# Modulation pieces and the latent attention's first projections take turns behind the recurrence

## The chip, the cores and the metric

The kernel runs on one core of one Trainium2 chip. The core's engines each work through a program of their own in order: TensorE (PE, the matmuls), VectorE (DVE), ScalarE (ACT), GpSimd (POOL) and SyncE (SP), whose queue issues the DMA transfers. They wait for each other through semaphores. The metric is the device time of one execution in microseconds (us), lower is better; the time of a kernel is the median of its runs.

## The reference

The reference is a trunk of two layers over 512 latent tokens and 256 context tokens of width 1024, in float32. Each layer normalises the tokens, scales and shifts them by a modulation vector, projects them once, gives the columns to four mixers, projects their outputs back and ends in a mixture of experts:

```python
for l in range(DEPTH):
    mod = sc @ w_ada[l] + b_ada[l]            # modulation, 6 * 1024 columns; modc likewise
    h = rmsnorm(x, norm1_g[l]) * (1 + s1) + sh1
    p = jnp.split(h @ w_in[l], split_at, axis=-1)
    o_a, oc_a = hgrn_mixer(p[0], ..., p[4], ...)           # gated recurrence, both directions
    o_b = hyena_mixer(p[5], *hy_args)                      # long convolution
    o_c, oc_c = na_mixer(p[6], ...)                        # neighbourhood attention
    o_d, oc_d = mla_mixer(p[7], p[8], p[9], ...)           # latent attention
    x = x + g1 * (jnp.concatenate([o_a, o_b, o_c, o_d], axis=-1) @ w_out[l])
    x = x + g2 * moe_ffn(rmsnorm(x, norm2_g[l]) * (1 + s2) + sh2, ...)
```

The change concerns three of these: the modulation `mod`, the recurrence `hgrn_mixer`, and the first projections of the latent attention, p[7] (256 columns) and p[8] (128 columns).

## The kernel before

The kernel is written in program order in Python; a scheduler then orders each engine's instructions. It keeps to what is written first where it can and fills gaps with what is written later, so the text sets priorities, and the order in which pieces are written sets the order in which they take up tiles of a shared pool.

**The recurrence** (`hgrn`). For two pairs of heads it first makes score tiles (L244), then goes through six levels. In a level, for each pair, ScalarE copies keys and queries into block order (L265), TensorE multiplies them (L237, 64-row matmuls into two large PSUM tiles `pa`), VectorE merges the result under a mask (L246) and multiplies the queries by the running decay (L272, L275), and POOL does the same with the keys (L273). The two pairs alternate. This is called the level loop below. Behind it, for each pair in turn, TensorE transposes the keys (L286) and multiplies them by the values (L299), VectorE runs a chain of 44 dependent small operations that carries the state over the blocks (L310, the state chain), and only then TensorE can make the outputs (L319, L322). The sum of squares (L328), ScalarE's square root by logarithm and exponential, and VectorE's last product (L332) close the pair. The result is written to memory by SP (`spill`).

**A modulation piece** (`Ada.step`, L1194). One of 24 column blocks of a layer's `mod`: two halves, each a 512 KB weight load that SP issues into a ring of three buffers (`araw`) and 4 small matmuls, which leave a 32-row result in a PSUM tile `pw`; ScalarE copies it out (L1199). After every eighth piece four matmuls sum the parts (L1204), VectorE adds the bias (L1209) and SP writes the row to memory (L1211). A half's load can be issued only when the half three before it has been multiplied.

**A projection** (`Proj.cols`, L1300). SP loads a 512 KB block of 128 columns (L1291), ScalarE rounds it to its high part (L1275), POOL makes the low part (L1276). TensorE multiplies high by high, high by low and low by high: 24 wide matmuls over the 512 latent tokens and, where the context is needed, 24 narrow ones over its 256 tokens. Each result is a PSUM tile `pw`; there are two such tiles, shared with the pieces, and they are given out in the order in which the code is written. Weight parts have two buffers. After each projection `between` adds the pieces that the list `STEPS` (layer 0) or `STEPS1` (layer 1) names for its number; behind the recurrence these are one piece after each of the projections named `cq`, `ckv` and the first three named `u` in layer 0, and none in layer 1.

In the code before, behind the call of `hgrn` stands `more(STEPH1 if l else STEPH)`: ten pieces in layer 0, thirteen in layer 1. Then come the projections `cq` (two) and `ckv` of the latent attention, which in layer 1 take `cq` over the latent tokens alone, and after them the six projections `u` of the long convolution.

Of the kernel before, what the change touches and what calls it, by code (L numbers as in the profile page):

```python
# [1347 lines left out]
ARAW1 = 3  # L1348
B0 = 1
STEPS1 = [1] * 2  # L1350
STEPH1 = 13
HLM = 2
FIRST = (12, 16)
FLIGHT = 5
LAG = 2
AHEAD = 1
STEPS = [1] * 8 + [0] * 2 + [1] * 6
STEPH = 10
CHUNK = 2048


# [41 lines left out]
def trunk(tc, d, out):  # L1403
# [7 lines left out]
    with ExitStack() as top:  # L1411
# [84 lines left out]
        def more(n, late=0):  # L1496
            for _ in range(n):
                if not adas[0].step(aring) and (l or late or adas[1].done < 8):
                    if adas[1].step(aring) and adas[1].done == 8:
                        adas[1].cols(n1g[1], mcs[1], mcb[1])  # L1500

        for l in range(2):
# [63 lines left out]
            def spill(group, tiles):  # L1566
                for k, o in enumerate(tiles):
                    nc.sync.dma_start(od[l][2 * group + k], o[:, :NQ])
# [1 line left out]
            E.cur = hg  # L1570
            ho = out_tiles()
            hgrn(E, full, QQ, F, K, V, SG, gn[:, 0:1], ho)
            more(STEPH1 if l else STEPH)
            spill(0, ho)


# [2 lines left out]
            ckv = E.t("mckv", NTOK, bufs=1)  # L1579
            for i in range(2):  # L1580
                pr.cols(COL["cq"] + i, both, lambda ps, a, n: nc.scalar.copy(cq[i][:, a:a + n], ps))
            pr.cols(COL["ckv"], PARTS, lambda ps, a, n: nc.scalar.copy(ckv[:, a:a + n], ps))
            hg.close()


# [194 lines left out]
            for c in range(4):  # L1780
# [3 lines left out]
                for t in range(nt + LAG * (c == 3)):  # L1784
                    if t < nt:
                        tt, cc = slice(t * P, (t + 1) * P), slice(c * 256, c * 256 + 256)
                        ps = E.pw()
                        i = 0
# [164 lines left out]
```

## Time and profile before

| | us |
|---|---|
| median of 3 runs | 2409.76 |
| lowest and highest run | 2402.96, 2412.77 |
| the profiled execution | 2422.56 |
| its span in the trace | 2420.7 |
| TensorE busy | 2043.4 (84%) |
| VectorE busy | 994.1 (41%) |
| level loop of layer 0 | 64.69 |
| from there to the end of the first projection `u` over the latent tokens | 52.65 |
| level loop of layer 1 | 46.86 |
| from there to the first third of the same projection | 51.48 |

The profiled execution took 12.8 us more than the median, so a difference worked out from its rows is applied to the median. The last four lines are the stretches in which the order of instructions changes. They are bounded by TensorE's instructions: the level loop goes from its first scores in a row to the first transposes of keys (L286). In rows of the timeline, xN counts TensorE's instructions as the profile does, and these matmuls take two each for the pieces and the recurrence.

### The profile page before, as it was taken

The numbers are of one execution on the slowest core, as the hardware profiler recorded it, in microseconds if no ns is written. First come the engines' busy times: TensorE is split into PE (matmuls) and PEld (weight loads), VectorE is DVE, ScalarE is ACT, GpSimd is POOL, SyncE is SP. The second block draws the span as 40 slices with busy tenths as digits, with TensorE's granted clock in tenths as the row PEclk, the third lists the DMA queues.
The fourth block names the chain that finished last, engine by engine and source line by source line (L and its number), as shares of the span: only waits on it lengthen the run. The fifth ranks groups of instructions, "written<-read, shape, count | busy, mean of one in ns | idle before, by whom it ended". The sixth has DMA issues, their size and how long they took to land. (4 is left out here: it accounts for less than half of the span.)

```text
span 2420.7 us, 32212 instructions
## 1 busy us (share of the span) xinstructions
PE 2043.4 (84%) x11540; PEld 1190.1 (49%) x11540; DVE 994.1 (41%) x2435; ACT 572.0 (24%) x1138; POOL 539.5 (22%) x429
## 2 busy tenths in 40 slices
PE   5789999899999588887777598999899598877776
PEld 1458688765688233322222386685669333222221
DVE  6751754647746422222112427555683511111111
ACT  3433432244622100000000234324351100000000
POOL 1652413211013122211111225131102221211111
PEclk9999899999998799999999799999998699999998
DMA  6434443202243899999999535520243899999996
GB/s 246 160 120 177 162 144 121 94 9 69 85 143 123 305 381 382 409 396 408 398 399 406 184 96 171 183 72 18 87 134 113 313 398 409 411 406 410 409 407 253
DMA packets 139310, 581.52 MB, mean 240 GB/s; under 512 B 23984, under 2 KB 47873, under 8 KB 88630
## 3 DMA queue, kind: packets, MB, share of 16 engines
q1 hardware_dynamic: 124054, 555.89, 59.5%
q0 software_dynamic: 15008, 22.36, 3.9%
q8 instruction: 151, 2.47, 0.4%
q14 instruction: 97, 0.79, 0.1%
HBM read 554.17 MB, written 36.80 MB: 244 GB/s over the span
## 5 line engine op out<-in xcount | busy, mean ns | idle before, releaser
L1012 PE MATMUL pb<-side,arena 128*64 128x512 f32 x1224 | 287.2, 603 | 42.7 <-DMA side<-in_w_moe 39.2
L1012 PE MATMUL pb<-arena 128*64 128x512 f32 x920 | 217.1, 604 | 36.5 <-DMA arena<-in_w_moe 33.0
L1016 DVE COPY arena<-pb 128x512 f32<-128x512 f32 x67 | 46.3, 691 | 490.7 <-PE pb L1012 490.7
L1028 ACT ACTIVATE arena<-pb 128x256 f32<-128x256 f32 x67 | 25.8, 384 | 899.9 <-PE pb L1025 899.9
L1276 POOL TENSOR_TENSOR wl<-side,wh 128x1024 fp32r<-128x1024 f32 x52 | 126.7, 2437 | 380.7 <-ACT wh L1275 252.1
L1012 PEld LDWEIGHTS pb<-side,arena 128*64 128x64 f32 x1224 | 81.7, 137 | 241.7 <-issue 128.9
L1300 PE MATMUL pw<-hh,wh 128*128 128x512 f32 (+1 forms) x720 | 166.1, 364 | 2.6 <-ACT arena L1644 1.3
L1043 DVE SCALAR_TENSOR_TENSOR arena<-pb,arena 128x512 f32<-128x512 f32 x67 | 50.3, 751 | 270.8 <-PE pb L1039 260.6
L1300 PE MATMUL pw<-hl,wh 128*128 128x512 f32 (+1 forms) x720 | 161.1, 358 | 0.0
L1039 PE MATMUL pb<-side,arena 128*64 128x512 f32 x576 | 140.5, 625 | 23.8 <-DVE arena L1029 22.0
L1300 PE MATMUL pw<-hh,wl 128*128 128x512 f32 (+1 forms) x720 | 159.0, 355 | 0.0
L1012 PEld LDWEIGHTS pb<-arena 128*64 128x64 f32 x920 | 61.9, 138 | 185.3 <-issue 99.5
L1052 POOL DMA_INDIRECT acc<-arena x35 | 55.2, 1578 | 385.8 <-DVE arena L1047 339.0
L1300 PEld LDWEIGHTS pw<-hh,wh 128*128 128x128 f32 x720 | 118.8, 191 | 35.1 <-issue 11.8
L1039 PE MATMUL pb<-arena 128*64 128x512 f32 x496 | 115.8, 606 | 23.5 <-DVE arena L1029 20.7
L1300 PEld LDWEIGHTS pw<-hh,wl 128*128 128x128 f32 x720 | 117.3, 189 | 25.8 <-issue 10.5
L1300 PEld LDWEIGHTS pw<-hl,wh 128*128 128x128 f32 x720 | 117.7, 189 | 24.6 <-issue 8.9
L1052 POOL DMA_INDIRECT out_dram<-arena x32 | 50.9, 1590 | 311.0 <-DVE arena L1043 296.9
L990 POOL DMA_INDIRECT arena<-h2d,arena x67 | 69.9, 1043 | 187.7 <-issue 75.6
L1795 POOL TENSOR_TENSOR arena<-arena 128x256 f32<-128x256 f32 x40 | 31.3, 783 | 301.1 <-DVE arena L1794 293.3
L1039 PEld LDWEIGHTS pb<-side,arena 128*64 128x64 f32 x576 | 39.7, 141 | 102.7 <-issue 60.7
L1025 PE MATMUL pb<-ident,arena 128*128 128x128 f32 x268 | 42.3, 280 | 55.4 <-DVE arena L1016 55.4
(367 smaller groups left out, 3442.5 us busy)
## 6 DMA issues: line engine op xcount, KB each, us to landing
side<-in_w_moe SPq DMA_DIRECT2D x215, 1024.0 KB, 13.6
arena<-in_w_moe SPq DMA_DIRECT2D x169, 1024.0 KB, 13.4
arena<-in_w_ada SPq DMA_DIRECT2D x53, 512.0 KB, 3.6
side<-in_w_in SPq DMA_DIRECT2D x52, 512.0 KB, 3.5
side<-in_w_ada SPq DMA_DIRECT2D x43, 512.0 KB, 4.0
arena<-in_w_out SPq DMA_DIRECT2D x16, 512.0 KB, 5.0
arena<-in_x SPq DMA_DIRECT2D x12, 512.0 KB, 5.6
spd<-arena SPq DMA_DIRECT2D x23, 256.0 KB, 2.4
```

What stands on the lines that cost most here:

```text
L990: E.gathered = nc.gpsimd.indirect_dma_start(out=xg, out_offset=None, in_=h2d, in_offset=bass.IndirectOffsetOnAxis(ap=gi, axis=0), **(dict( ...
L1012: nc.tensor.matmul(pg[64 * s:64 * s + 64], xT[:, j // 4, j % 4, :], W[j // 2][:, (j % 2) * 1024 + s * 512:(j % 2) * 1024 + s * 512 + 512], ...
L1016: nc.vector.tensor_copy(gu, pg)
L1025: nc.tensor.transpose(pt[:, c * 128:(c + 1) * 128], gu[:, c * 128:(c + 1) * 128], E.c["ident"])
L1028: nc.scalar.activation(hT, pv[:, :, 0, :], AF.Silu)
L1039: nc.tensor.matmul(pd[64 * s:64 * s + 64], hT[:, c, :], W[4 + c // 2][:, (c % 2) * 1024 + s * 512:(c % 2) * 1024 + s * 512 + 512], start=( ...
L1043: nc.vector.scalar_tensor_tensor(y, pd, w[0], g2[0], op0=ALU.mult, op1=ALU.mult)
L1052: E.nc.gpsimd.indirect_dma_start(out=acc, out_offset=bass.IndirectOffsetOnAxis(ap=si, axis=0), in_=y, in_offset=None, compute_op=ALU.add, ...
L1276: (nc.vector if k % 2 else nc.gpsimd).tensor_sub(lo, src, hi.bitcast(F32))
L1300: nc.tensor.matmul(ps[:, :n], w[:, j, :], h[:, j, a:a + n], start=(i == 0), stop=(i == 23))
L1795: nc.gpsimd.tensor_add(x1[t][:, cc], x1[t][:, cc], tmp)
```

## The change

After `hgrn` no piece is written any more. Instead the pieces stand behind the three projections of the latent attention: 3, 3 and 4 in layer 0, 4, 4 and 5 in layer 1. With those of `STEPS` that is 4, 4 and 5 in both layers. The number of pieces, of projections and of everything else stays the same.

```diff
-STEPH1 = 13
-STEPH = 10
+STEPH = ((3, 3, 4), (4, 4, 5))
...
             hgrn(E, full, QQ, F, K, V, SG, gn[:, 0:1], ho)
-            more(STEPH1 if l else STEPH)
             spill(0, ho)
...
             for i in range(2):
                 pr.cols(COL["cq"] + i, both, lambda ps, a, n: nc.scalar.copy(cq[i][:, a:a + n], ps))
+                more(STEPH[l][i])
             pr.cols(COL["ckv"], PARTS, lambda ps, a, n: nc.scalar.copy(ckv[:, a:a + n], ps))
+            more(STEPH[l][2])
             hg.close()
```

Outside the two stretches every engine's order is the same as before; from the next projection on TensorE's rows are identical.

On TensorE, in the level loop of layer 0 (`pa` are the recurrence's score tiles, L1194 a piece, L1300 a projection with `wh`, `wl` its weight parts and `hh`, `hl` the parts of the tokens), this is the middle of the loop:

```order
+L1300 MATMUL pw_2215<-hh_502,wl_2212 128x512
+L1300 MATMUL pw_2241<-hh_502,wh_2211 128x256 x6
+L237 MATMUL pa_1704<-arena 128x128 x4
+L237 MATMUL pa_1705<-arena 128x128 x4
 L237 MATMUL pa_1704<-arena 128x128
 L237 MATMUL pa_1705<-arena 128x128
-L1194 MATMUL pw_2268<-side_343,csil 32x256 x5
+L237 MATMUL pa_1704<-arena 128x128
+L237 MATMUL pa_1705<-arena 128x128
+L1300 MATMUL pw_2241<-hh_502,wh_2211 128x256 x2
+L1300 MATMUL pw_2241<-hl_503,wh_2211 128x256 x6
```

Between the scores of two levels there now stand matmuls of the first `cq` projection where a piece stood. In the whole loop ten pieces and a sum with 9 wide matmuls of `cq` became all of the first `cq`, four pieces and 7 wide matmuls of the second. In the loop of layer 1 nine pieces and a sum became the 24 wide matmuls of the first `cq`, four pieces and 2 wide matmuls of the second.

On TensorE behind the loop of layer 0, for the second pair of heads, this stood between the products of keys and values (L299) and the outputs (L319, L322) that need the state chain:

```order
L299 MATMUL pa_2080<-arena 128x64 x12
L299 MATMUL pa_2119<-arena 128x64 x12
L1300 MATMUL pw_2482<-hl_503,wh_2478 128x512
L1300 MATMUL pw_2482<-hh_502,wl_2479 128x512 x8
L1300 MATMUL pw_2508<-hh_502,wh_2478 128x256 x8
L1300 MATMUL pw_2508<-hl_503,wh_2478 128x256 x8
L1300 MATMUL pw_2508<-hh_502,wl_2479 128x256 x8
L1194 MATMUL pw_2534<-arena,csil 32x256 x4
L1194 MATMUL pw_2534<-side_343,csil 32x256 x4
L1300 MATMUL pw_2553<-hh_502,wh_2549 128x512 x8
L1300 MATMUL pw_2553<-hl_503,wh_2549 128x512 x5
L319 MATMUL pa_2158<-arena 64x128
```

and this stands there now:

```order
L299 MATMUL pa_2080<-arena 128x64 x12
L299 MATMUL pa_2119<-arena 128x64 x12
L1300 MATMUL pw_2434<-hl_503,wh_2430 128x512 x2
L1300 MATMUL pw_2434<-hh_502,wl_2431 128x512 x8
L1300 MATMUL pw_2460<-hh_502,wh_2430 128x256 x8
L1300 MATMUL pw_2460<-hl_503,wh_2430 128x256 x8
L1300 MATMUL pw_2460<-hh_502,wl_2431 128x256 x8
L1194 MATMUL pw_2486<-side_343,csil 32x256 x8
L1194 MATMUL pw_2498<-arena,csil 32x256 x4
L319 MATMUL pa_2158<-arena 64x128
L322 MATMUL pa_2158<-arena 64x64 x2
L319 MATMUL pa_2158<-arena 64x128
```

The 13 wide matmuls of the first `u` projection went behind the pair's outputs, and half a piece and one wide matmul of `ckv` came in. Behind the outputs there now stand three and a half pieces in a row, and then `u`. For the first pair the matmuls in this place are 14 wide and 24 narrow ones of the second `cq` with one and a half pieces; for the two pairs of layer 1 they are 18 wide matmuls, two pieces and a sum, and then one wide and 24 narrow matmuls with two pieces. In layer 1 before, the first of these places held three pieces and most of a sum, and nothing else.

On POOL, in layer 1 (L273 is the recurrence's product of the keys, by level; L1276 the low part of a projection's weights), the level loop now holds one weight split:

```order
 L273 TENSOR_TENSOR arena<-arena 128x96x4 x4
 L273 TENSOR_TENSOR arena<-arena 128x48x8 x4
+L1276 TENSOR_TENSOR wl_16934<-side_15490,wh_16933 128x1024
 L273 TENSOR_TENSOR arena<-arena 128x24x16 x4
 L273 TENSOR_TENSOR arena<-arena 128x12x32 x4
-L1276 TENSOR_TENSOR wl_17003<-side_15490,wh_17002 128x1024
 L1276 TENSOR_TENSOR wl_17062<-side_15490,wh_17061 128x1024
 L1276 TENSOR_TENSOR wl_17095<-side_15490,wh_17094 128x1024
```

The split of `ckv` moved from behind the loop to the place between two of its levels. The same happens in layer 0, and ScalarE's rounding of the same weights (L1275) moves with it. On SP, in layer 1, the load of the projection weights that reuses this block's buffer moved ahead of the pieces' loads of the loop.

## Rows read from the trace of the kernel before

**Rows 1.** The page, its first line: the span of the profiled execution.

```profile
span 2420.7 us, 32212 instructions
```

**Rows 2.** Windows: from:to, length, busy PE, PEld, DVE, ACT, POOL, clock, DMA share, GB/s.

```profile
242.72:307.41 64.69, 58.73 (x561) 43.96 (x561) 50.99 (x77) 25.20 (x63) 27.50 (x33) 0.87 0.51 176
...
307.41:360.06 52.65, 52.12 (x481) 42.33 (x479) 28.06 (x97) 20.52 (x33) 7.59 (x3) 1.00 0.33 111
...
1465.36:1512.22 46.86, 39.59 (x410) 27.08 (x409) 40.44 (x77) 20.13 (x60) 27.63 (x33) 0.93 0.60 199
...
1512.22:1563.70 51.48, 46.19 (x400) 33.90 (x397) 28.01 (x99) 18.14 (x34) 7.39 (x3) 0.97 0.46 155
```

**Rows 3.** Timeline of VectorE, layer 0's level loop: start, length, [idle before <-releaser].

```profile
266.04 1.94 DVE L246 COPY_PREDICATED arena<-hmask,pa 128x768 f32<-128x768 uint32 x2 [1.36 <-PE pa L237]
...
281.56 1.94 DVE L246 COPY_PREDICATED arena<-hmask,pa 128x768 f32<-128x768 uint32 x2 [4.23 <-PE pa L237]
...
298.26 0.68 DVE L1209 TENSOR_TENSOR arena<-pw,arena 128x512 f32<-128x512 f32 x1
```

**Rows 4.** Timeline of TensorE, layer 0's level loop: two of its waits.

```profile
257.07 3.63 PE L237 MATMUL pa<-arena 64*128 64x128 f32 x24 [1.78 <-DVE arena L246]
...
277.66 0.62 PE L1194 MATMUL pw<-side,csil 128*32 128x256 f32 x2 [3.30 <-DMA side<-in_w_ada]
```

**Rows 5.** Timeline behind layer 0's loop: TensorE, and VectorE's state chain.

```profile
309.61 2.90 PE L299 MATMUL pa<-arena 64*128 64x64 f32 x48
...
311.22 11.15 DVE L310 SCALAR_TENSOR_TENSOR arena<-arena,pa 64x64 f32<-64x64 f32 x44 [3.24 <-PE pa L299]
...
324.21 0.27 PE L322 MATMUL pa<-arena 128*64 128x64 f32 x1
...
327.29 1.20 PE L1300 MATMUL pw<-hh,wl 128*128 128x512 f32 x4
```

**Rows 6.** Timeline of TensorE, layer 0: a piece, then a projection's halves.

```profile
373.50 1.07 PE L1194 MATMUL pw<-side,csil 128*32 128x256 f32 x16
...
396.41 2.00 PE L1300 MATMUL pw<-hh,wh 128*128 128x512 f32 x8
...
401.87 1.12 PE L1300 MATMUL pw<-hh,wh 128*128 128x256 f32 x8
...
404.75 2.00 PE L1300 MATMUL pw<-hh,wh 128*128 128x512 f32 x8
```

**Rows 7.** Loads of the pieces' weights in layer 0, from issue to landing.

```profile
DMA to landing us min/median/max: 3.3/4.7/6.3
```

**Rows 8.** Timeline of VectorE, POOL and TensorE, layer 1.

```profile
1511.32 1.35 DVE L246 COPY_PREDICATED arena<-hmask,pa 128x512 f32<-128x512 uint32 x2 [2.51 <-PE pa L237]
...
1549.98 2.39 POOL L1276 TENSOR_TENSOR wl<-side,wh 128x1024 fp32r<-128x1024 f32 x1 [5.07 <-PE pw L1300]
...
1517.57 1.07 PE L1194 MATMUL pw<-arena,csil 128*32 128x256 f32 x16
...
1530.86 1.67 PE L1300 MATMUL pw<-hh,wh 128*128 128x512 f32 x6
...
1530.97 0.69 DVE L1209 TENSOR_TENSOR arena<-pw,arena 128x512 f32<-128x512 f32 x1 [3.79 <-PE pw L1204]
```

**Rows 9.** Timeline of two more waits of TensorE, and windows behind four waits.

```profile
483.80 0.70 PE L748 MATMUL pb<-arena,ones 128*128 128x256 f32 x2 [2.14 <-DVE arena L194]
...
484.00:488.00 4.00, 4.00 (x19) 3.12 (x18) 3.05 (x7) 0.68 (x2) 0.00 (x0) 1.00 0.00 0
...
1721.82 4.11 PE L806 MATMUL pa<-arena 128*128 128x512 f32 x6 [2.35 <-ACT arena L599]
...
1722.00:1728.00 6.00, 6.00 (x15) 3.03 (x16) 5.38 (x11) 1.98 (x4) 3.32 (x2) 0.72 0.25 82
...
257.00:268.00 11.00, 10.93 (x74) 8.16 (x74) 9.18 (x14) 3.62 (x9) 4.65 (x6) 0.55 0.30 109
...
278.00:284.00 6.00, 6.00 (x43) 4.29 (x42) 2.44 (x4) 1.95 (x5) 1.36 (x2) 0.54 0.04 10
```

## The prediction

> **What bounds the kernel now.** I read the page first for the span [rows 1], then cut the two places whose order changes into windows, and read the timeline of each engine inside them. The rest of the kernel keeps its order, so the time changes by what these four stretches gain or lose, 215.7 us of 2420.7 in all [rows 1, 2]. The reader is to see two kinds of stretch. Behind the loop of layer 0 TensorE is busy for 52.12 of 52.65 us at full clock: TensorE is the bound, every wait put there costs its whole length, and there is only 0.53 us of idle time to win. In the level loop of layer 0 neither engine is full: TensorE shows 58.73 of 64.69 us, but at a mean clock of 0.87, and VectorE 50.99 [rows 2]. The loop is a chain between the two, and it stalls in places: VectorE waits 4.23 us before 281.56, because TensorE had waited 3.30 us for the second half of a piece's weights and then ran the next scores at a low clock [rows 3, 4, 9]. The loop of layer 1 is bound by VectorE (40.44 of 46.86 us) until its end, where VectorE waits 2.51 us for scores [rows 2, 8]. Behind that loop TensorE has little to do but pieces while the state chain runs, and waits for their weights.
>
> **Prices.** Without waits a piece costs TensorE 1.0 us, 24 wide matmuls 5.46 us (396.41 to 401.87), 24 narrow ones 2.88 us (401.87 to 404.75) [rows 6]. A sum's eight matmuls are not shown without a neighbour; I take 1.6 us, since each is as long in columns as two of a piece's, which makes it 1.0 by the piece's price if they overlap as well and up to 2 if not. A state chain ends at 322.37 (311.22 + 11.15), and the products L299 ahead of it at 312.51, so TensorE has 9.9 us to fill before the outputs can be made [rows 5].
>
> **A, level loop of layer 0: -4.4 us.** The work that fills it stays the same: before ten pieces, a sum and 9 wide matmuls, 10 + 1.6 + 2.0 = 13.6 us; now 8.34 for a whole projection, four pieces and 7 wide matmuls, 13.9 us. But where the piece waited for its weights there now stand matmuls whose weights were split ahead of the loop, and the four pieces come in its last third, three halves loaded in advance. So I take away the 4.23 us, and the 0.68 us of the modulation's addition on VectorE [rows 3], which moves behind the loop: -4.9. Against it stands the split of `ckv`'s weights on POOL, 2.39 us a piece of work [rows 8], now between two levels. POOL is busy for 27.50 of 64.69 us here [rows 2], so most of it falls in gaps; between 0 and 2.4 I take 0.5, near the lower end. The other low stretch of the clock, 257 to 268, begins behind a wait of 1.78 us that ends on VectorE [rows 4, 9], which the change doesn't touch, so I leave it. If it went, VectorE would win perhaps 2 us more (the wait of 1.36 at 266.04 [rows 3] and smaller ones).
>
> **B, behind the loop of layer 0: +5.9 us.** What filled the 9.9 us of each pair was a projection's worth and the start of the next. Now the first pair has 14 wide and 24 narrow matmuls and one and a half pieces, 3.2 + 2.9 + 1.5 = 7.6 us, and the second 10 wide, 24 narrow and one and a half pieces, 2.3 + 2.9 + 1.5 = 6.7 us. TensorE then stands in its order before outputs that need the chain: 2.3 and 3.2 us of waiting, less 0.5 each for the first output matmuls, which need only the pair's first half: 4.5 us. What is late next is the pieces behind them: a half lands 4.7 us after its issue (3.3 to 6.3) [rows 7] and is issued when the half three before it has been used. Behind the second chain three halves lie ready, and four more follow. The outputs (3.08 us, 324.21 to 327.29 [rows 5]), the sum of squares (1.2) and the halves in between cover about one landing, and the last two loads, issued about 4 us after the chain's end, are waited for about 1.5 us together; the first pair's pieces I give 0.7. That makes 2.2 us (0.8 with the fastest landing, 5 with the slowest). The work itself shrinks: six pieces and a sum come (7.6), 22 wide and 24 narrow matmuls go into the loop (5.0 + 2.9): -0.3. The idle 0.53 us of before goes. Sum 4.5 + 2.2 - 0.3 - 0.5 = +5.9, from +4.5 to +8.7.
>
> **D, level loop of layer 1: -1.5 us.** VectorE's wait of 2.51 us at the end [rows 8] mostly goes with the pieces' load that held TensorE there (-2.0), and the addition (-0.7). The split on POOL, which is busy for 27.63 of 46.86 us in this loop [rows 2], is worse here than in layer 0: half of its 2.39 us, +1.2. From -2.7 to +0.4 (all of the split, and half of the wait kept). On SP the load that waits for this split now stands ahead of the pieces' loads; three halves are in the ring by then and the first is used in the second half of the loop, so I cost that at nothing; if the split came 3 us later, the loop would wait about as long.
>
> **E, behind the loop of layer 1: 0.** From L299's end at 1517.57 to 1530.86 TensorE needed 13.3 us for three and a half pieces and a sum, 5.1 us of work, and 0.4 of first outputs: 7.8 lost, waiting for weights, and VectorE's addition waited 3.79 us for the sum with the last step of the chain queued behind it [rows 8]. Now the first place holds 18 wide matmuls, two pieces and a sum: 4.1 + 2.0 + 1.6 = 7.7 of 9.9 us, 1.7 of waiting. The second holds 0.2 + 2.9 + 2.0 = 5.1: 4.3 of waiting, under which the weights of the next piece load. The five pieces at the end add 1.0, and the work grows by 0.7 (five pieces and a sum, 6.6, for 26 wide matmuls, 5.9). Together 7.7 against 7.8: nothing, from -3.8 (the addition's wait alone is won) to +2.
>
> **F, the clock: +2.5 us.** TensorE now waits about 2 to 4 us four times. Behind a wait of 2.14 us the clock stayed at 1.00; behind one of 2.35 it was 0.72 for 6 us, behind 3.30 it was 0.54 for 6 us, behind 1.78 it was 0.55 for 11 us [rows 4, 9]; these are mixtures of the two levels, 1.2 and 2.4 GHz. Lost full-speed time is 0, 1.7, 2.8 and 5.0 us. I take a fall behind two of the four waits at 2 us each, +4, less the 0.03 of 51.48 us, 1.5, that the stretch in layer 1 already loses [rows 2]. [...]
>
> **The sum.** -4.4 + 5.9 - 1.5 + 0 + 2.5 = +2.5 us: the profiled execution would go from 2422.6 to 2425.1, and the median, 12.8 us below it, from 2409.8 to **2412**. A run of this kernel varies by some 5 us either way, and 0.5% (12 us) is about what a measurement can tell from no change. So the forecast is no change: what the loops gain is given back behind them.
>
> **Rivals.**
> *Faster.* The loops win and the waits are harmless: A -6.9 (the other low stretch goes, POOL's split is free), B +4.5, D -2.7, E -3.8, F -1.5 together -10.4 us: 2399. For it speaks that layer 0's worst stall is taken out for certain; against it that behind that loop TensorE has no idle time to give [rows 2], so that each uncovered microsecond of a chain shows. To pass 0.5% it needs the chain waits covered too. Chance 0.16.
>
> *Slower.* The clock falls behind all four chain waits and stays low for as long as behind 257 [rows 9], 5.0 us each: F = 20 - 1.5 = 18.5, and the total is +18.5: 2428. It decides from the third such fall on (15 - 1.5 gives +13.5). For it: two of three waits over 2 us in these rows were followed by a fall. Against it: the work ahead of the waits is dense, and in three of the four they are below 3 us. Chance 0.22.
>
> *The weights bind.* The clumps of four and five pieces wait for loads at the slow landing, 6.3 us: B +8.7, E +2, total +7.3: 2417, still within 0.5%. Chance 0.15; the forecast itself 0.47. Together 0.62 for no change, and the range reaches into both outer cases: 2397 to 2427.
>
> **What would show it.** Right: layer 0's loop shorter by 3 to 7 us with no wait for piece weights in its first half; TensorE waiting 1.5 to 3 us for VectorE before the outputs (L322) of both pairs there; L1276 inside both loops; behind layer 1's first chain no long wait for weights. Wrong: the stretch behind layer 0's loop no longer than 53 us, or the clock at 1.00 through all four chains (then the faster rival), or below 0.8 in both stretches behind the loops (then the slower one).

## The result, and the profile after

The changed kernel takes 2432.6 us (median of 5 runs, 2427.3 to 2436.1) beside 2412.3 us of the kernel before on the same chip (5 runs, 2403.0 to 2418.1): a ratio of 1.008 [1.006, 1.010]. It is about 20 us slower, where I had forecast no change (2412, up to 2427). The profiled execution after took 2427.29 us.

The same four stretches as in [rows 2], between the same instructions, by the windows of the changed kernel (columns as there), and behind them eight shorter windows:

```profile
241.49:298.15 56.66, 52.17 (x502) 43.25 (x502) 49.74 (x76) 25.05 (x60) 29.48 (x34) 1.00 0.27 94
298.15:365.56 67.41, 56.12 (x538) 39.49 (x537) 34.86 (x104) 21.94 (x37) 4.73 (x2) 0.97 0.58 194
1465.42:1515.53 50.11, 43.46 (x348) 32.04 (x347) 43.63 (x76) 20.32 (x58) 30.10 (x34) 0.83 0.27 88
1515.53:1569.70 54.17, 48.01 (x459) 31.60 (x458) 31.59 (x105) 18.58 (x37) 4.74 (x2) 0.97 0.65 232
...
298.15:309.47 11.32, 11.32 (x102) 9.99 (x100) 7.53 (x31) 6.25 (x10) 0.00 (x0) 1.00 0.01 3
...
298.15:356.00 57.85, 47.46 (x498) 33.96 (x496) 31.51 (x101) 21.19 (x35) 4.73 (x2) 1.00 0.53 177
312.00:316.00 4.00, 2.29 (x48) 1.74 (x45) 1.02 (x4) 0.37 (x1) 0.12 (x1) 1.00 0.96 345
336.00:340.00 4.00, 4.00 (x31) 3.67 (x29) 3.50 (x15) 1.44 (x2) 0.00 (x0) 1.00 0.02 6
352.00:356.00 4.00, 1.03 (x15) 0.31 (x14) 3.02 (x4) 1.69 (x2) 0.00 (x0) 1.00 0.99 328
356.00:360.00 4.00, 3.10 (x27) 0.97 (x19) 3.35 (x4) 0.37 (x1) 0.00 (x0) 0.70 0.83 272
...
1499.00:1511.00 12.00, 12.00 (x81) 8.41 (x81) 9.89 (x22) 5.83 (x21) 5.46 (x6) 0.50 0.53 162
1556.00:1560.00 4.00, 4.00 (x39) 2.15 (x39) 0.76 (x3) 0.37 (x1) 0.00 (x0) 0.61 0.71 176
```

Layer 0's loop is shorter, 56.66 us for 64.69. Behind it TensorE's time without work goes from 0.53 us (52.65 less 52.12) to 11.29 us (67.41 less 56.12), and its busy time grows by 4.0. Layer 1 loses on both sides of its loop's end. What the idle time behind layer 0's loop waits for, by the list of TensorE's waits from 242 to 362 (us in total, times, longest), where the first, third, fourth and fifth lines lie behind the loop and add up to 11.2 us:

```profile
PE pw L1194 <- DMA side<-in_w_ada: 6.3, 5, 3.0
PE pa L237 <- DVE arena L246: 4.1, 5, 1.7
PE pa L319 <- DVE arena L310: 2.2, 2, 1.7
PE pw L1204 <- ACT arena L1199: 1.8, 1, 1.8
PE pw L1194 <- DMA arena<-in_w_ada: 0.9, 1, 0.9
```

The timeline of the changed kernel's TensorE shows one clump of pieces around the end of the first chain and the other around the end of the second:

```profile
309.47 0.64 PE L1194 MATMUL pw<-side,csil 128*32 128x256 f32 x8
309.93 0.61 PE L1194 MATMUL pw<-arena,csil 128*32 128x256 f32 x8
310.36 0.61 PE L1194 MATMUL pw<-side,csil 128*32 128x256 f32 x8
313.85 0.64 PE L1194 MATMUL pw<-side,csil 128*32 128x256 f32 x8 [1.71 <-DMA side<-in_w_ada]
...
327.44 1.04 PE L1204 MATMUL pw<-arena,sum 128*32 128x512 f32 x2 [1.82 <-ACT arena L1199]
...
340.00 1.07 PE L1194 MATMUL pw<-side,csil 128*32 128x256 f32 x16
340.89 0.61 PE L1194 MATMUL pw<-arena,csil 128*32 128x256 f32 x8
343.25 0.40 PE L319 MATMUL pa<-arena 128*64 128x128 f32 x2 [1.75 <-DVE arena L310]
...
355.61 0.64 PE L1194 MATMUL pw<-side,csil 128*32 128x256 f32 x8 [2.97 <-DMA side<-in_w_ada]
357.15 0.67 PE L1194 MATMUL pw<-arena,csil 128*32 128x256 f32 x8 [0.90 <-DMA arena<-in_w_ada]
357.75 1.22 PE L1300 MATMUL pw<-hh,wh 128*128 128x512 f32 x2
...
363.75 1.98 PE L1300 MATMUL pw<-hh,wl 128*128 128x512 f32 x8
```

The reader is to see the transfers' rhythm. While TensorE runs the second `cq` (298.15 to 309.47) the ring holds its three halves and the DMA engines stand idle, at a share of 0.01. Then TensorE uses the three halves up in 1.5 us, and while it waits for more the transfers run full: 345 GB/s at a share of 0.96 from 312 to 316. Under the second chain it repeats itself: from 336 to 340 the share is 0.02, then three halves go by 341.5, and from 352 to 356 the rate is 328 GB/s at 0.99. At that rate the 1 MB of a piece needs 3 us (1.05 MB by 345 GB/s), where its matmuls need 1.0 us [rows 6]. In the old order scores stood between the pieces, and the transfers ran through the loop, at a mean of 176 GB/s [rows 2].

In layer 1's loop, the timelines of VectorE, POOL and TensorE of the changed kernel:

```profile
1489.61 1.59 DVE L272 TENSOR_TENSOR arena<-arena 128x256 f32<-128x256 f32 x2
1491.13 0.32 DVE L275 TENSOR_TENSOR arena<-arena 128x48 f32<-128x48 f32 x2
...
1492.60 3.37 DVE L272 TENSOR_TENSOR arena<-arena 128x256 f32<-128x256 f32 x2
1495.90 1.66 DVE L275 TENSOR_TENSOR arena<-arena 128x48 f32<-128x48 f32 x2
...
1498.69 0.74 DVE L272 TENSOR_TENSOR arena<-arena 128x256 f32<-128x256 f32 x2
```

```profile
1493.14 2.55 POOL L1276 TENSOR_TENSOR wl<-side,wh 128x1024 fp32r<-128x1024 f32 x1
1495.64 1.85 POOL L273 TENSOR_TENSOR arena<-arena 128x384 f32<-128x384 f32 x2
1501.51 1.84 POOL L273 TENSOR_TENSOR arena<-arena 128x384 f32<-128x384 f32 x2 [4.02 <-ACT arena L265]
```

```profile
1498.24 2.07 PE L237 MATMUL pa<-arena 64*128 64x128 f32 x13 [3.32 <-DVE arena L246]
```

While POOL splits `ckv`'s weights, VectorE's products L272 take 3.37 us, and the products L275 behind them, which now meet POOL's L273 of 1495.64, take 1.66; the same shapes one step earlier took 1.59 and 0.32. TensorE waits 3.32 us for VectorE, and the granted clock is 0.50, the lower of its two levels, for the next 12 us (window above).

### The profile page after: what moved, and what is told of

The parts are those of the page before. It is cut to its first block, busy times and chain, and to the rows that moved or that the text cites. A ratio compares the mean times of both kernels' runs of the same rounds, so it can differ in the third digit from the quotient of the medians.

```text
span 2425.4 us, 32209 instructions
## 1 busy us (share of the span) xinstructions
PE 2039.1 (84%) x11540; PEld 1183.5 (49%) x11540; DVE 994.3 (41%) x2435; ACT 572.8 (24%) x1138; POOL 537.6 (22%) x429
## 5 line engine op out<-in xcount | busy, mean ns | idle before, releaser
L1276 POOL TENSOR_TENSOR wl<-side,wh 128x1024 fp32r<-128x1024 f32 x52 | 126.2, 2426 | 403.6 <-ACT wh L1275 252.6
L1300 PE MATMUL pw<-hh,wh 128*128 128x512 f32 (+1 forms) x720 | 169.0, 367 | 4.3 <-DVE arena L495 2.4
L1300 PE MATMUL pw<-hl,wh 128*128 128x512 f32 (+1 forms) x720 | 160.6, 357 | 0.0
L1300 PE MATMUL pw<-hh,wl 128*128 128x512 f32 (+1 forms) x720 | 159.6, 356 | 0.0
L1052 POOL DMA_INDIRECT acc<-arena x35 | 55.2, 1577 | 385.4 <-DVE arena L1047 338.1
L1300 PEld LDWEIGHTS pw<-hh,wh 128*128 128x128 f32 x720 | 118.6, 192 | 39.3 <-issue 16.9
L1300 PEld LDWEIGHTS pw<-hh,wl 128*128 128x128 f32 x720 | 117.2, 189 | 26.2 <-issue 10.5
L1300 PEld LDWEIGHTS pw<-hl,wh 128*128 128x128 f32 x720 | 117.9, 190 | 24.6 <-issue 8.4
```

Source lines behind the costliest of these rows:

```text
L1052: E.nc.gpsimd.indirect_dma_start(out=acc, out_offset=bass.IndirectOffsetOnAxis(ap=si, axis=0), in_=y, in_offset=None, compute_op=ALU.add, ...
L1276: (nc.vector if k % 2 else nc.gpsimd).tensor_sub(lo, src, hi.bitcast(F32))
L1300: nc.tensor.matmul(ps[:, :n], w[:, j, :], h[:, j, a:a + n], start=(i == 0), stop=(i == 23))
```

## The experiments

Three theories went into them (where an expectation uses their letters, these are not the prediction's steps). **Weights (A):** clumps of four and five pieces use up the ring of three halves and then wait for transfers. **Cover (B):** the projections no longer stand under the state chains. **Split (C):** the split of `ckv`'s weights on POOL, between two levels, slows layer 1's loop. Each ratio is to the kernel before on the same chip. The stretches of the table are read from the traces: the loops from the first L237 to the first L286 of the layer, "behind" from there to the first L748 in layer 0 and the first L806 in layer 1.

| kernel | ratio [95%] | loop 0 | behind 0 | loop 1 | behind 1 |
|---|---|---|---|---|---|
| before | 1 | 64.7 | 165.1 | 46.9 | 194.0 |
| the change | 1.008 [1.006, 1.010] | 56.7 | 179.3 | 50.1 | 197.0 |
| l0_only | 1.0060 [1.0041, 1.0078] | 59.7 | 180.6 | 44.6 | 191.5 |
| l1_only | 1.0053 [1.0034, 1.0072] | 59.8 | 163.7 | 50.0 | 204.2 |
| split_dve | 1.0066 [1.0046, 1.0086] | 55.2 | 179.1 | 45.2 | 197.8 |
| after_noload | 1.0009 [0.9994, 1.0023] | 56.7 | 162.6 | 47.5 | 189.4 |
| before_noload | 0.9981 [0.9968, 0.9995] | 58.6 | 168.2 | 45.7 | 187.8 |
| l0_clump_u | 1.0061 [1.0037, 1.0084] | 59.6 | 186.3 | 44.6 | 191.4 |
| l0_thin | 1.0038 [1.0022, 1.0053] | 59.8 | 173.6 | 45.4 | 193.6 |
| l0_thin_late | 1.0048 [1.0034, 1.0062] | 60.6 | 174.1 | 44.5 | 195.6 |
| l0_thin_act | 1.0027 [1.0014, 1.0041] | 56.9 | 170.6 | 44.7 | 194.2 |
| l1_thin | 1.0024 [1.0012, 1.0037] | 57.4 | 163.8 | 50.6 | 195.4 |
| thin_split | 1.0022 [1.0011, 1.0033] | 55.1 | 174.7 | 45.2 | 195.2 |
| thin_split_act | 1.0013 [1.0002, 1.0025] | 55.2 | 169.0 | 45.2 | 193.9 |
| before_act | 1.0012 [0.9999, 1.0024] | 62.2 | 165.4 | 44.3 | 196.8 |
| ring_3_4 | 1.0092 [1.0077, 1.0107] | 56.9 | 180.5 | 49.9 | 196.5 |
| before_ring_4 | 0.9996 [0.9980, 1.0012] | 59.2 | 164.1 | 46.4 | 195.1 |

**One layer at a time.** `l0_only` and `l1_only` keep the new order in one layer and put the other layer's pieces back behind `hgrn`:

```diff
-STEPH = ((3, 3, 4), (4, 4, 5))
+STEPH = ((3, 3, 4), (0, 0, 0))     # l1_only: ((0, 0, 0), (4, 4, 5))
...
+            more(13 if l else 0)   # l1_only: more(0 if l else 10)
             spill(0, ho)
```

> The new order in layer 0 alone, layer 1 as before. The stretches of the two traces say that layer 0 loses 6.7 us (loop 8.0 shorter, the part behind it 14.8 longer) and layer 1 about 8. Theory A, that the loss is the pieces' weights, late behind a ring of three halves, and theory B, that it is the projections that left the shadow of the state chains, both expect about 7 us over the kernel before: 2419, with the stretch behind the loop at 66 to 68 us. Theory C, that the loss is POOL's split between the levels, which slows VectorE in layer 1, expects nothing here: 2412.

> The new order in layer 1 alone. From the stretches: loop 3.2 longer, the part behind it 2.7, and 2.4 of a wait behind that: 2420. Theory C expects all of the loss of the change here, 2425 to 2432, with VectorE's L272 between the levels at 3 us for two where it took 1.4; theory B expects 2 to 4 us, since chains lose their cover here less.

Measured: 2421.83 and 2422.46 us beside 2408.8, 13.0 and 13.7 us. Each layer does its own harm; together the two are more than the 20.3 us of the whole change, at the edge of what the intervals leave. That layer 0 alone loses so much rules out the split of layer 1's loop as the whole cause, and 13.7 us in layer 1 are far over the 2 to 4 of the cover. The 7 us that were expected of `l0_only` were read from the one pair of profiles and fell 6 short. `l1_only` shows a reason: its layer 0 is in the old order, and that loop took 59.83 us, not 64.69, with 0.3 us of waits for piece weights. Over the six kernels of the table with the old order in layer 0 it took 57.4 to 64.7, and [rows 2] is the longest of them.

**The split on VectorE.** The change, with `ckv`'s low weight part made by VectorE:

```diff
-    def cols(self, c, parts, evac):
+    def cols(self, c, parts, evac, k=0):
...
-        split_r(E, wh, wl, raw, 0)
+        split_r(E, wh, wl, raw, k)
...
             pr.cols(COL["ckv"], PARTS, ..., 1)
```

> The changed kernel with the low part of the ckv weights made by VectorE instead of POOL, in both layers; nothing is left out. Theory C: layer 1's loop goes from 50.1 back to 46 or 47 us and the low clock in it goes; the time is 3 to 6 us below the changed kernel's 2433. If the split only fills gaps, as the prediction had it: 2433 or a microsecond more.

Measured: 2424.57 us, 15.8 over before on its chip, some 4.5 us less than the 20.3 of the change, though the intervals of the two ratios overlap. (The 8 us that an expectation below takes for the split is the difference of two medians taken apart, beside which the kernel before took 2412.3 and 2408.8.) The table is plainer: layer 1's loop takes 49.9 to 50.6 us in the four kernels that have the split there on POOL with the loads in place, and 45.2 in all three that have it on VectorE. Layer 0's loop shows it too: 55.1 to 55.2 in these three, 56.7 to 60.6 in the seven with the new order, the loads and the split on POOL. VectorE's timeline of `split_dve` at the same level of the loop, with the split as an instruction of its own:

```profile
1494.46 1.59 DVE L272 TENSOR_TENSOR arena<-arena 128x256 f32<-128x256 f32 x2
1495.98 0.32 DVE L275 TENSOR_TENSOR arena<-arena 128x48 f32<-128x48 f32 x2
...
1498.82 1.22 DVE L1276 TENSOR_TENSOR wl<-side,wh 128x1024 fp32r<-128x1024 f32 x1
```

and the window that had the low clock:

```profile
1499.00:1511.00 12.00, 8.73 (x97) 6.05 (x90) 10.85 (x24) 7.57 (x27) 7.33 (x8) 1.00 0.74 266
```

The split costs VectorE 1.22 us, the products are back at 1.59 and 0.32, and the clock stays at 1.00 (this loop begins 4.9 us later; from 1503.9 to 1515.9 it is 1.00 as well).

**Without the loads.** The pieces behind the three projections without their loads; and the control, the kernel before without the loads of the pieces behind `hgrn`:

```diff
-            nc.sync.dma_start(wt, self.w[c, half])
+            if not self.dry:
+                nc.sync.dma_start(wt, self.w[c, half])
...
-                more(STEPH[l][i])
+                dry(STEPH[l][i])           # more() with dry set
-            more(STEPH[l][2])
+            dry(STEPH[l][2])               # before_noload: dry(STEPH1 if l else STEPH)
```

> The changed kernel without the weight loads of the pieces that stand behind the three projections (10 in layer 0, 13 in layer 1); they multiply what lies in the ring, so the modulation is not the reference's. The scheduler, which counts on the loads, may place these pieces earlier. Theory A: the 8 us of waits for weights behind each loop go, and the time falls by 12 us or more, to 2420 or below. Theory B: the pieces stay behind the chains and the time falls by less than 5 us.

> The kernel before without the loads of the ten and thirteen pieces behind the recurrence (their products are made from what the ring holds, so the modulation's values are left out): the control for the changed kernel without the loads of the same pieces, which took 1.0009 of before. Theory of the weights: the old order hardly waits for them (0.3 us in layer 0, 4.3 in layer 1), so it loses 2 to 5 us, ratio 0.998 to 0.999, and without loads the two orders are within 0.3% of each other. Theory of the cover: the old order is the better one by itself and stays over 10 us ahead without loads too, ratio 0.996 or less.

Measured: 2411.87 us, 1.0009, for the new order and 2407.25, 0.9981, for the old one. The loads are worth 0.0071 to the change and 0.0019 to the kernel before; the difference, 0.0052 or 12.5 us, is what they cost the new order more; from the three intervals I estimate that it can be some 7 us off either way. The weights theory expected both runs. Without them the new order is still 0.0028, some 7 us, behind. The runs have a flaw: with cheap pieces the scheduler itself puts more of them under the chains (in `after_noload` five pieces stand under layer 0's second chain, where the change has one and a half), so a part of the 12.5 us may be that order.

**Where the clump stands.** Layer 0's four added pieces of `ckv` behind the first `u`, which brings 12 wide matmuls of `u` back under the second chain:

```diff
-STEPS = [1] * 8 + [0] * 2 + [1] * 6
-STEPH = ((3, 3, 4), (4, 4, 5))
+STEPS = [1] * 8 + [0] * 2 + [1] * 3 + [5, 1, 1]
+STEPH = ((3, 3, 0), (0, 0, 0))
...
+            more(13 if l else 0)
             spill(0, ho)
```

> Layer 1 is as before; in layer 0 the four added pieces behind ckv stand behind the first u projection instead, five in a row there. The matmuls of u come back under the second state chain, where layer 0's change alone (+13.0 us, 1.006) had none. Theory of the cover (the loss is the chains' time left empty): the loss shrinks by the 2.3 us of chain waits and the part of u that ran behind the chain, to about +8, ratio 1.003. Theory of the weights (the loss is clumps that empty the ring of three halves): the clump only moves, TensorE waits 5 to 6 us for piece weights in layer 0 as it did, now behind u, and the time stays within 3 us of layer 0's change alone: +10 to +13, ratio 1.004 to 1.006.

Measured: 2427.21 us, 17.0 over before, beside 13.0 of `l0_only`. The chain waits fall from 2.3 to 0.5 us, as the cover wants, and it is no faster: the clump waits 4.7 us for transfers behind `u`, and TensorE 3.7 us for VectorE in the long convolution (L518), a wait that neither theory had. So the time lies above both forecasts. The cover alone is not the loss.

**Spread pieces.** In layer 0 four pieces stand behind the first `cq` and one or two behind each later projection; in layer 1 four, three and two, and then single ones. This was done in layer 0 alone, in layer 1 alone, and in both with the split on VectorE:

```diff
+STEPS = [1] * 8 + [0] * 2 + [1] * 3 + [2, 2, 2, 1, 1]     # layer 0
+STEPS1 = [1] * 2 + [0] * 11 + [1] * 4                     # layer 1
+STEPH = ((3, 1, 1), (4, 3, 2))
```

> Layer 1 is as before; in layer 0 the sixteen pieces are spread: four behind the first cq, two each behind the second cq, ckv and the first three u, one each behind the next two. Theory of the weights: no clump behind the loop empties the ring, the 6.2 us of waits for piece weights, the 1.8 us for ScalarE's copy and the clock's fall behind them go, and of the +13.0 us of layer 0's change some +3 remain, ratio 1.001. Theory of the cover: u stands under the second chain again, but the spread pieces push the projections back all the same; the chain waits of 2.3 us go and the rest stays, +10, ratio 1.004.

> Layer 0 is as before; in layer 1 the thirteen pieces are spread: four, three and two behind cq, cq and ckv, one each behind the first four u. Layer 1's change alone cost +13.7 us (1.0053). Theory of the weights: the 5.3 us of waits for piece weights go, the rest stays, +8, ratio 1.0035. Theory of the split (POOL's part of ckv's weights between two levels slows VectorE, and the clock falls behind it): that split stays in the loop, so the loop is 50 us long as it was and at least +8 stays; if the pieces' loads queued behind that split on SP are what counts, little of the 13.7 goes, +12.

> Both layers with the spread pieces, and ckv's low weight part made by VectorE, not POOL. Weights and split together: layer 0 keeps some +3, layer 1 loses the 8 us that the split cost the changed kernel and the 5 us of waits, about +0 to +5 against before, ratio 1.000 to 1.002, against +20 (1.008) of the change. If the two effects are one (the queue on SP behind the split), the sum of the gains is smaller: +10, ratio 1.004. Cover: +12, ratio 1.005.

Measured: 2418.36, 2416.26 and 2415.14 beside 2410.2 us. The waits for weights are gone from layer 0, but only some 5 of its 13 us come back, which is the figure of the cover though of the chain waits only 0.4 us are left. In layer 1 the waits for weights behind the loop fall from 5.3 to 2.2 us, the wait for a tile there (2.4 us) goes, and 7.6 of 13.7 us come back, with the loop still at 50.6. With both layers spread and the split on VectorE 4.9 us are left. In layer 0 there is now a new wait, in TensorE's timeline of `l0_thin`:

```profile
358.94 1.94 PE L1194 MATMUL pw<-side,csil 128*32 128x256 f32 x16 [4.42 <-issue]
```

The trace names no releaser. VectorE's timeline of the same kernel suggests one:

```profile
354.32 0.96 DVE L194 TENSOR_SCALAR arena<-pa 128x768 f32<-128x768 f32 x1 [6.03 <-PE pa L328]
355.31 0.96 DVE L331 TENSOR_TENSOR arena<-pa,arena 128x768 f32<-128x768 f32 x1
356.18 1.13 DVE L494 SCALAR_TENSOR_TENSOR arena<-pw,arena 128x511 f32<-128x511 f32 x2
357.23 0.95 DVE L197 TENSOR_TENSOR arena<-arena 128x768 f32<-128x768 f32 x1
358.10 0.74 DVE L495 SCALAR_TENSOR_TENSOR arena<-pw,arena 128x511 f32<-128x511 f32 x1
```

The first `u` is ready at about 345, but the convolution that empties its `pw` tile (L494, L495) stands behind the second pair's norm in VectorE's order, and the norm waits for the outputs. There are two such tiles. In the order before, the pair's outputs ran ahead of the end of this projection.

**Is it the tile?** First the piece behind that `u` was moved away, then ScalarE was made to copy the results of the first two `u` out of their tiles (with the spread pieces in layer 0, in both layers with the split on VectorE, and in the kernel before as control):

```diff
-STEPS = [1] * 8 + [0] * 2 + [1] * 3 + [2, 2, 2, 1, 1]
+STEPS = [1] * 8 + [0] * 2 + [1] * 3 + [0, 2, 2, 2, 1, 1]      # l0_thin_late
```

```diff
+                def ev(ps, a, n):
+                    if full and i < 2:
+                        s = E.t("ustage", 512, bufs=2)[:, :n]
+                        nc.scalar.copy(s, ps)
+                        ps = s
+                    short_conv(E, uc[n][i], ps, n, cw[:, i])
```

> Layer 0's spread pieces (1.0038 of before), with none behind the first u and two behind the fourth instead. In the spread version the piece behind the first u waited 4.4 us, and the clock was at 0.50 for 4 us after it. If that wait is for a result tile that VectorE empties late (the two short convolutions of u stand between its operations of the pair's norm), both go, 6 us less, and the ratio is 1.001 to 1.002. If the spread pieces push the other work back in any order, the wait turns up in another place and the ratio stays at 1.0035 to 1.004.

> Layer 0's spread pieces (1.0038 of before), and in layer 0 ScalarE copies the results of the first two u projections out of their tiles, so that they come free before the second pair's norm; the short convolutions then read the copies. Theory of the tile: the wait of 4.4 us behind the first u goes, with the low clock behind it, 6 us: ratio 1.001 to 1.002, and no wait over 1 us for L495 or for a piece's tile between 350 and 362. Rival, the spread order is longer whoever empties the tiles: 1.0035 to 1.005.

> All three causes taken out: the pieces spread in both layers, ckv's split on VectorE, and ScalarE's copies of the first two u results in layer 0. The version without the copies took 1.0022 of before. If weights, split and tile are the whole loss, it comes within 3 us of before: ratio 0.999 to 1.001. If a part of the loss lies in the order itself, 1.002 or more.

> The kernel before with ScalarE's copies of the first two u results in layer 0: the control for the copies by themselves. There TensorE reaches these tiles later and does not wait for them, so the tile theory expects no change, ratio 0.999 to 1.001. If the copies are worth something of their own, 0.998 or less.

`l0_thin_late`, 2424.03 us, is slower than either theory had it, and tells who was waiting: now it is the next projection, in TensorE's timeline,

```profile
358.90 3.75 PE L1300 MATMUL pw<-hh,wh 128*128 128x512 f32 x8 [4.47 <-DVE arena L495]
```

with the releaser named. It was the tile, and whoever needs it next stands there. With the copies the wait is gone:

```profile
352.11 0.63 PE L1194 MATMUL pw<-arena,csil 128*32 128x256 f32 x6
352.67 2.11 PE L1300 MATMUL pw<-hh,wh 128*128 128x512 f32 x8
355.56 0.64 PE L1194 MATMUL pw<-side,csil 128*32 128x256 f32 x8 [0.79 <-DMA side<-in_w_ada]
```

That moved the time less than I expected: 1.0027 from 1.0038, with overlapping intervals, though the stretch behind loop 0 is 3 us shorter. The copies themselves seem to cost something, 1.0012 [0.9999, 1.0024] in the kernel before. `thin_split_act`, at 1.0013 or 4.2 us over before, fell between its two theories (within 3 us, or 1.002 and more). Against the control with the copies it loses nothing: with the spread pieces, the split on VectorE and the tiles freed early, the new order is as fast as the old one with the same copies, and no faster.

**A larger ring.** Four halves in layer 1, in the change and in the kernel before:

```diff
-ARAW1 = 3
+ARAW1 = 4
```

> The change with a ring of four halves instead of three in layer 1 alone; layer 0's memory has no room for a fourth. In the changed kernel TensorE waits 5.2 us for piece weights behind layer 1's loop. Theory that the ring of three is what the clumps empty: one more half in advance takes about one landing of 3 us off those waits, and the time is 3 us below the change: ratio to before 1.0065 to 1.007 where the change has 1.008. Rival: in a clump the transfers themselves are full (the DMA share was 0.96 to 0.99 there), so a fourth half only shifts the wait, and the ratio stays at 1.008.

> The kernel before with four halves in layer 1's ring. There TensorE waits 4.3 us for piece weights behind layer 1's loop. If the ring of three sets these waits, 2 to 4 us go: ratio 0.9985, a version that is ahead of both kernels by less than 0.5%. If the transfers are full, ratio 1.000.

Measured: 1.0092, no better than the change, and 0.9996. TensorE's waits behind layer 1's loop in `ring_3_4`, and its longest wait there in `before_ring_4`:

```profile
PE pw L1194 <- DMA arena<-in_w_ada: 5.8, 3, 3.5
...
PE pa L299 <- ACT arena L289: 2.1, 1, 2.1
```

With the change's clumps one more half in advance takes nothing off the waits, which fits transfers that are full already. In the order before, it takes away all of the 4.3 us behind the loop (1.9 us of waits for weights are left inside it), and a wait of 2.1 us for ScalarE's copy L289 has come; the time doesn't show the gain. No version that does the whole work beats the kernel before by what can be measured.

## Why the prediction was wrong

The forecast of no change, at most 2427 us, failed in two steps of its sum: B priced the waits for piece weights at 2.2 us where they took 7.2, and D took 1.5 us off a loop that lost 5.0, because the split was priced on POOL alone.

**A, loop of layer 0, -4.4.** The profiled pair gives -8.0, but the profiled execution before was a long one here: without it the old order takes 57.4 to 62.2 (five kernels), the new one with POOL's split 56.7 to 60.6 (seven): about -1 between the means. The stall that I took away, 3.30 us for a piece's weights and 4.23 on VectorE, is 0.3 to 1.9 us of waits for weights in the four other old-order kernels with their loads. And the split, in the sum at +0.5, is worth more: with it on VectorE the loop takes 55.1 to 55.2. I applied the difference of a profile that lay 12.8 us above the median to the median; a stall of the one execution was counted as if all had it.

**B, behind it, +5.9.** It measured +14.8 (67.41 less 52.65), and by the table +15.5 between the means of five old-order kernels (163.7 to 165.4) and of four with the change's order (179.1 to 180.6). This is the step that failed by most. The terms: waits for piece weights 7.2 us where I had 2.2 (0.8 to 5); chain waits 2.2 (0.48 and 1.75) where I had 4.5; the sum's wait for ScalarE 1.8, which I did not have: a piece's copy (L1199) stood behind ScalarE's four copies L303. About 2.0 are clock (67.41 us at a mean of 0.97), and some 2 more of busy time I can't assign. The weights were priced by the landing of one load, 4.7 us, with the work around it as cover, and with three halves ready behind the second chain. But the piece and a half that I had put under that chain were these three halves: TensorE used them up there (340.00 to 341.50), and the loads behind them were issued from 340.70 on. And four pieces in a row ask for 1 MB in each microsecond of TensorE's work, and the transfers give a third of that. That the ring had stood full for 11 us before, with the transfers idle, was in the order shown with the change, and I did not read it as lost transfer time.

**D, loop of layer 1, -1.5.** It measured +3.2 in the profiled pair, +5.0 by the table (a mean of 50.2 for the four kernels named above, 45.2 for eight old-order kernels with the loads). The split was in the sum at +1.2, half of its 2.39 us as time of POOL. It should have been priced on VectorE, whose products lost 1.8 us beside the split (3.37 for 1.59) and 1.3 beside the L273 that it had pushed back (1.66 for 0.32), and at the clock behind it. `split_dve` shows both. The -2.0 had no ground either: in the timeline before, the load held TensorE for 0.49 us only,

```profile
1503.99 1.08 PE L1194 MATMUL pw<-arena,csil 128*32 128x256 f32 x8 [0.49 <-DMA arena<-in_w_ada]
```

and in the changed kernel VectorE still waits 0.95 and 1.42 us for the last scores.

**E, behind it, 0.** +2.7 in the profiled pair, and a wait of 2.40 us for a `u` tile right behind, at 1581.35: the upper end of my bound, +2, and more. `l1_only`, with the same order in layer 1, took 204.2 us there, 10 more than before, with the clock at a mean of 0.97 for 0.99. The chain waits of 1.7 and 4.3 us did not come: the pieces at the end of the first chain wait 1.19 and 0.54 us for weights, those of the second 2.61 and 0.69, and the outputs then find the chain done.

**F, the clock, +2.5.** The mechanism was wrong. I had falls behind two chain waits. The chain waits in layer 0, at most 1.75 us, left the clock at 1.00 up to 356; four falls stand behind other waits, 2.97 us for weights (0.70 from 356 to 360), 2.61 and 0.69 for weights in layer 1 (0.61 from 1556 to 1560), and in layer 1's loop 3.32 for VectorE (0.50 for 12 us) and 1.30 for VectorE (0.60 from 1473 to 1477). The Trainium skill, "TensorE: Matmul & The Clock Gate", section "HAM oscillation — how this bites in real kernels", describes bursts of matmuls that each begin at the half clock because a long wait for transfers lies ahead of each. The falls behind the two waits for weights agree with it; behind shorter waits both happen here (1.30 and 1.75 us).

**The sum and the rivals.** Loop 0 about -1, behind it +15.5, loop 1 +5.0, behind it +3.5 (197.0 and 196.5 with the whole change, a mean of 193.2 for the five old-order kernels with the loads, three halves and no copies; +5.6 if `split_dve` and `l1_only` are counted in): +23 to +25, where the medians gave +20.3. By cause: the loads some 12.5 us more than in the old order, the split some 5; that the rest, about 3 us, is chain waits and tiles is not shown. The rival of the slower side came near in time, 2428, by luck: its cause, the clock at four chain waits, did not happen. The rival in which the weights bind had the right mechanism, at +8.7 for what took nearly twice that: it bounded a clump by the slowest single landing, 6.3 us.

## What to carry to other kernels

Price a run of loads by its rate: bytes that it needs while the engine works through it, against what the transfers give when full, and look for the time ahead of it in which the ring is full and they idle. Work that is spread among a loop's gaps keeps the transfers going (176 GB/s through layer 0's loop before); the same work in a clump let them stand and then waited for them, and a buffer more did not mend that here. And take a stall from a profile only if a second execution has it too, above all when that profile lies off the median.

## What the runs showed of the hardware

An elementwise product on VectorE depends on what POOL does beside it. Two products L272 (128x256) took 0.74 us with POOL idle (1498.69), 1.59 beside POOL's L273, and 3.37 beside its weight split L1276, which itself took 2.55 us for 2.39 elsewhere [rows 8]. The split costs VectorE 1.22 us when VectorE makes it, less than the 1.78 (3.37 less 1.59) that it loses when POOL does. The Trainium skill, "Trainium Architecture — The Big Picture", section "🎯 What this means for kernel authors", says that VectorE and GpSimd contend for one shared pair of ports and that it is an exclusive lock, not a division of their rate. The trace agrees: the slow pair ends at 1495.97 (1492.60 and 3.37), 0.28 us behind the end of the split (1493.14 and 2.55), and took 2.63 us more than with POOL idle, a part of it beside the L273 ahead of the split.
